# A hybrid encoder layer: the mixers' pieces put into the stream of dense products in twos, or alone after a time

## The chip, the cores and the metric

The kernel runs on one NeuronCore of a Trainium2 chip. The metric is the device time of one execution in microseconds (us). The core has TensorE (PE: matrix products; PEld is its weight load), VectorE (DVE), ScalarE (ACT), GpSimd (POOL) and SyncE (SP, which here issues most of the DMAs). They run their own queues of instructions and wait for each other by semaphores.

## What is computed

One layer of a streaming encoder, for a prompt of 1024 tokens and 8 samples of 16 tokens, 1152 columns in all, at a model width of 1024:

```python
def trunk_layer(x, mem_k, mem_v, ...):
    y, ... = hybrid_mixer(rms_norm(x, norm_mix_w), ...)     # x @ W_in -> 4 mLSTM + 4 gated-DeltaNet heads -> @ W_out
    x = x + y
    x = x + memory_cross_attention(rms_norm(x, norm_x_w), mem_k, mem_v, wq_x, wo_x)
    x = x + squared_relu_mlp(rms_norm(x, norm_ffn_w), w_ff1, w_ff2)

def hybrid_mixer(xn, ...):
    proj = xn @ w_in
    ...
    (C1, n1, m1), h = lax.scan(mlstm_chunk_step, carry0, ...)
    ...
    S1, o = lax.scan(gdn_chunk_step, S0, ...)               # delta rule: a triangular solve in each chunk
    ...
    y = jnp.concatenate([h_a, h_b], axis=-1) @ w_out
```

All is float32. The big ("dense") products are made of fp32r products of a high and a low part of each operand, three of them for one product; the mixers' own small products are plain fp32.

## The kernel before

The activations lie with features on partitions and the 1152 columns in three blocks of 384. A dense product of one chunk of 128 output features is `project` (line 377): for each block, `dense` (line 235) makes eight steps of three matmuls of 128x128 by 128x384 into one PSUM bank. A chunk thus has 24 dense steps, and its weights are loaded and split one chunk ahead (`chunks`, line 1902).

The order of the work is written out by a planner. `Driver` (line 72) holds a clock `t` and a list of tasks; a task is a Python generator that emits instructions and yields `(pe, delay)`: the time on TensorE that it has just emitted, and how long its next step should stay away until its inputs are there. `stream` (line 103) takes the dense steps one by one; each yields `3 * n / 2360.0` (line 257), which moves `t` on, and then `run_ready` (line 83) runs every task that is due. Such a step of a task is called a piece here. Where the dense stream itself can't go on, it yields WAIT, and `skip` (line 96) moves `t` to the next task that is due. Two things make it wait: a flag (`wait`, line 218) and slots. All long-lived tiles are slots of one pool of 34; `room_s` (line 149) holds a chunk until enough are free, with a reserve for heads that have started, and tasks poll in `room` (line 144) and `until` (line 223).

The building framework then orders the instructions of each engine itself, by priority (which is the order of emission, with `hp()` ahead) and by when it thinks an instruction's inputs are ready.

The stream of the stage that the change touches is one call (line 1994). In it come, after an opening of three chunks: for each head the projections of a delta-rule ("gdn") head, three chunks with a short convolution, and of an mLSTM head, three chunks, with the two heads' gate chunks some chunks later; then the memory keys (`mem_k`, line 1094, which waits for the flag `rm`) and values; then the first seven of eight chunks of W_out for block 0. As tasks run:
- `gates` (line 460): the gates' cumulative sums for all heads;
- `gdn` (line 681), one head after the other: 6 transposes (delay 0.5), a pause of 2.0, 9 score steps (0.4), pauses of 0.8 and 0.2, 3 transposes (0.4), a pause of 4.5, 15 steps of a substitution on DVE alone (`yield 0.0, 0.6`), pauses of 5.0 and 0.8, 6 steps of a block inverse (1.0 to 1.2), 6 steps of products with it (0.2 and 0.4), and the state pass over 9 tiles (steps of 0.8 and 0.4 in turn);
- `mlstm` (line 964), one head after the other, from when its three chunks are projected: 16 steps of transposes and scores (0.4 and 0.5), 13 of a state pass (0.2 to 0.6);
- `head_out` (line 937): the head's normalisation, three output transposes, once the gate chunk is there;
- `conv_act` (line 619): three steps after each convolution chunk;
- `mem_in` (line 1068), spawned two chunks ahead of `mem_k`: once nine slots are free, it loads the memory tokens (line 1077), splits and squares them in eight steps of delay 0.8 (lines 1083 to 1087), and sums and spreads the row factor; then it sets `rm`.

The last gate chunk frees 17 slots (line 665). PSUM has three banks for the dense products and five for the pieces (`psd`, `psm`).

Of the kernel before, what the change touches and what calls it, by code (L numbers as in the profile page):

```python
# [64 lines left out]
A_Q, A_S, A_P, A_T, A_X = 2.5, 0.5, 3.0, 1.5, 3.5  # L65
X_DELAY = (0.0, 9.5, 18.0)
WAIT, BREAK = -1.0, -2.0
MIX_ORDER = (4, 0, 5, 1, 6, 2, 7, 3)
ORDER = [("g", 0), ("m", 0), ("g", 1), ("m", 1), ("g", 2), ("m", 2), ("g", 3), ("m", 3)]


class Driver:
# [2 lines left out]

    def __init__(self):
        self.t, self.tasks, self.n, self.idle = 0.0, [], 0, 0

    def spawn(self, gen, delay=0.0):
        self.n += 1  # L80
        self.tasks.append([self.t + delay, self.n, gen])

    def run_ready(self):
        while True:
            ready = [k for k in self.tasks if k[0] <= self.t]
            if not ready:
                return
            k = min(ready, key=lambda k: k[1])
            try:
                pe, delay = next(k[2])  # L90
                self.t += pe
                k[0] = self.t + delay
            except StopIteration:
                self.tasks.remove(k)

    def skip(self):
        assert self.tasks, "nothing can run"
        self.idle += 1
        assert self.idle < 20000, [k[2].__qualname__ for k in self.tasks]
        self.t = max(self.t, min(k[0] for k in self.tasks))  # L100
        self.run_ready()

    def stream(self, steps):
        for x in steps:
# [7 lines left out]
class Kern:  # L112
# [31 lines left out]
    def room(self, n):  # L144

        while NSLOT - self.live < n:
            yield 0.0, 0.4

    def room_s(self, n):

# [72 lines left out]
    def until(self, *flags):  # L223

        while not all(f in self.done for f in flags):
            yield 0.0, 0.5

    def mm3(self, ps, lh, ll, rh, rl, start, stop, more=False):

# [707 lines left out]
    def head_out(self, ov, sc, r, hd):  # L937
# [7 lines left out]
        for g in range(3):  # L945
# [7 lines left out]
            nc.sync.dma_start(self.mixD[:, hd, s], gate[:, s])  # L953
            if hd == MIX_ORDER[-1] and g == 0:
                while 0 not in self.mix:
# [194 lines left out]
    def mix_in(self, b):  # L1150
# [13 lines left out]
        self.x1[b] = lambda k: x1t[k // 3][:, k % 3]  # L1164
        left = [k for k in MIX_ORDER if b or k != MIX_ORDER[-1]]
        for k in left:
# [16 lines left out]
    def wout(self, b, f):  # L1183
        w = yield
        if f == 0:
            yield from self.wait(f"mixin{b}{MIX_ORDER[0]}")
        x1 = self.x1[b]
        yield from self.dense(
            w, self.mix[b], lambda ps: self.nc.vector.tensor_tensor(x1(f), ps[:, :BW], x1(f), ALU.add),
            order=MIX_ORDER, need=(lambda k: f"mixin{b}{k}"))  # L1190
        if f == KT - 1:
            self.F(6)
            self.dr.spawn(self.norm_x(b))
# [218 lines left out]
    def wo(self, b, f):  # L1412
        w = yield
        yield from self.wait(f"oin{b}0")
        x1 = self.x1[b]
        yield from self.dense(
            w, self.o[b], lambda ps: self.nc.vector.tensor_tensor(x1(f), ps[:, :BW], x1(f), ALU.add),
            need=lambda k: f"oin{b}{k}")
        self.done.add(f"wo{b}{f}")
        if f == KT - 1:  # L1420
            self.F(6)
# [545 lines left out]
    def build(self):  # L1967
        tc, nc, A, dr = self.tc, self.nc, self.A, self.dr
        self.x1g, self.x1, self.x1t, self.xn2, self.q, self.o, self.rs16, self.mix = {}, {}, {}, {}, {}, {}, {}, {}
        self.xq, self.xo, self.hid, self.E, self.fs, self.keep = {}, ({}, {}), {}, {}, {}, 4  # L1970
        wout = lambda b: [(A["wout"][f], self.wout(b, f)) for f in range(KT)]
        PS = bass.MemoryType.PSUM
        with ExitStack() as ps:
            dense = ps.enter_context(ExitStack())
            self.pd = dense.enter_context(tc.tile_pool(name="psd", bufs=3, space=PS))
            self.pm = dense.enter_context(tc.tile_pool(name="psm", bufs=5, space=PS))
            with tc.tile_pool(name="m1", bufs=2) as m1:
                self.m1 = m1
                self.consts()
                self.xh = [self.S([P, T], F32R, "xh") for _ in range(KT)]  # L1980
                self.xl = [self.S([P, T], F32R, "xl") for _ in range(KT)]
                self.rB = self.S([P, T], F32, "rB")
                w0 = wout(0)
                seq = self.mixers()
                dr.stream(self.opening(seq[:3], seq[3][0]))
                nc.sync.dma_start(self.cst, A["cst"][:, C_NEGP:])
                zero = self.S([P, NT, 32], F32, "zero")
                nc.gpsimd.memset(zero, 0.0)
                nc.sync.dma_start(self.yD.rearrange("t s i -> s t i"), zero)
                self.F()  # L1990
                seq = seq[3:]
                seq[-4] = (seq[-4][0], self.also(seq[-4][1], [(self.mix_in(0), 0.0)]))
                w0[2] = (w0[2][0], self.also(w0[2][1], [(self.mix_in(1), 0.0)]))
                dr.stream(self.chunks(seq + w0[:7], w0[7][0]))
                self.finish(*(f"mix{k}" for k in range(8)))
                nc.sync.dma_start(A["pconv_o"], self.pconv)
                nc.sync.dma_start(A["sconv_o"], self.sconv)
            m4 = self.m4 = ps.enter_context(tc.tile_pool(name="m4", bufs=2))
            wq = lambda b: [(A["wq"][f], self.wq(b, f)) for f in range(KT)]
            wo = lambda b: [(A["wo"][f], self.wo(b, f)) for f in range(KT)]  # L2000

            def at(items, i, *tasks):
                items[i] = (items[i][0], self.also(items[i][1], [(t, 0.0) for t in tasks]))
                return items

            with tc.tile_pool(name="m2", bufs=2) as m2:
                self.m2 = m2
                self.reserve = 0
                seq = w0[7:] + wout(1) + at(wq(0), 0, self.mix_in(2), self.sample_loads())
                seq += wout(2) + wq(1) + at(wq(2), 0, self.o_in(0), self.o_in(1), self.o_in(2))  # L2010
                last = wo(2)
                seq += at(wo(0), 0, self.ff_in(0)) + at(wo(1), 0, self.ff_in(1), self.ff_split(0))
                dr.stream(self.chunks(seq, last[0][0]))
                self.finish(*(f"at{b}3" for b in range(NB)))
            m3 = self.m3 = ps.enter_context(tc.tile_pool(name="m3", bufs=2))
            full = [p for p in range(16) if p not in FIRST]
            units = [(p, (0,)) for p in FIRST] + [(p, (0, 1)) for p in full] + [(p, (1,)) for p in reversed(FIRST)]
            self.left = [sum(a in blocks for _, blocks in units) for a in range(2)]
            hid, ws = {}, []
            jobs = []  # L2020
            for i, (p, blocks) in enumerate(units):
                plain = i < len(FIRST)
                jobs.append(((A["wff1"][2 * p], A["wff1"][2 * p + 1]), 512, TWO if plain else UP,
                             self.up_plain(p, 0) if plain else self.up(p, blocks)))
            start = {len(jobs) - len(FIRST): [self.feed()]}
            for u, (d, idx) in enumerate(DOWN_UNITS):
                src = A[f"wd{u}"].rearrange("p q n -> p (q n)")
                n = len(idx) * P
                if u == len(DOWN_UNITS) - 4:
                    start[len(jobs)] = [self.plain_in(hid), self.plain_w(ws)]  # L2030
                jobs.append(((src[:, :2 * n], src[:, 2 * n:]), n, DOWN, self.down(u)))
            ff = self.seven(jobs, start)

            def warm():
                next(ff)
                yield 0.0, 0.0

            dr.stream(self.chunks(at(at(last, 0, self.ff_in(2), self.ff_split(1)), 6, warm())))
            dense.close()
            self.pf = ps.enter_context(tc.tile_pool(name="psf", bufs=4, space=PS))  # L2040
            dr.stream(ff)
            self.F(2)
            self.x1 = [lambda f, b=b: self.E[f].rearrange("p a n t -> p (a n t)")[:, b * BW:(b + 1) * BW]
                       for b in range(NB)]
            dr.stream(self.ff2_last(ws, hid))
            while dr.tasks:
                dr.skip()
# [121 lines left out]
```

## Time and profile before

| | us |
|---|---|
| median of three runs | 1833.7 (1833.43 to 1834.89) |
| the profiled execution | 1834.41 |
| its span, first to last instruction | 1832.6 |
| TensorE busy in the span | 1773.2 |
| DVE busy | 1236.7 |
| ScalarE busy | 788.5 |
| POOL busy | 444.2 |

In a timeline a row is a run of instructions of one kind on one engine: its start, its length, the engine, the line of the kernel, the operation, the tile written and those read, the shape, how many there are, and in brackets the idle time of the engine before it and what ended it. Matmuls are pipelined, so a matmul's length overlaps the next one's; the beat is read from the starts. A plain fp32 product of 128 columns shows as two instructions (two passes).

### The profile page before, as it was taken

The numbers are of one execution on the slowest core, as the hardware profiler recorded it, in microseconds if no ns is written. First come the engines' busy times: TensorE is split into PE (matmuls) and PEld (weight loads), VectorE is DVE, ScalarE is ACT, GpSimd is POOL, SyncE is SP. The second block draws the span as 40 slices with busy tenths as digits, with TensorE's granted clock in tenths as the row PEclk, the third lists the DMA queues.
The fourth block names the chain that finished last, engine by engine and source line by source line (L and its number), as shares of the span: only waits on it lengthen the run. The fifth ranks groups of instructions, "written<-read, shape, count | busy, mean of one in ns | idle before, by whom it ended". The sixth has DMA issues, their size and how long they took to land. (4 is left out here: it accounts for less than half of the span.)

```text
span 1832.6 us, 32932 instructions
## 1 busy us (share of the span) xinstructions
PE 1773.2 (97%) x12938; PEld 1718.5 (94%) x12938; DVE 1236.7 (67%) x2243; ACT 788.5 (43%) x1690; POOL 444.2 (24%) x415
## 2 busy tenths in 40 slices
PE   7999899999999999999999989999999899999997
PEld 6998899998999999988999989999999799999996
DVE  7877656765675667544676687555556777867886
ACT  6334324315225465445665444444445633433433
POOL 3023213122112202020002454222223332222213
PEclk9999999999999999999999999999999899999999
DMA  4111221121112476796144533433335834533512
GB/s 174 55 56 44 73 77 54 52 76 62 65 53 90 152 264 218 247 323 233 59 162 148 187 110 106 146 142 138 143 142 177 287 119 142 169 121 121 168 42 104
DMA packets 100706, 242.91 MB, mean 133 GB/s; under 512 B 24736, under 2 KB 48192, under 8 KB 100552
## 3 DMA queue, kind: packets, MB, share of 16 engines
q1 hardware_dynamic: 100256, 240.62, 38.7%
q8 instruction: 102, 1.67, 0.4%
q14 instruction: 52, 0.43, 0.1%
q10 hardware_dynamic: 296, 0.19, 0.0%
HBM read 182.87 MB, written 57.91 MB: 131 GB/s over the span
## 5 line engine op out<-in xcount | busy, mean ns | idle before, releaser
L231 PE MATMUL d<-xh,wh 128*128 128x384 f32 x944 | 342.1, 362 | 1.1 <-DVE k L458 0.6
L233 PE MATMUL d<-xh,wl 128*128 128x384 f32 x944 | 320.6, 340 | 0.3 <-DVE wl L212 0.3
L232 PE MATMUL d<-xl,wh 128*128 128x384 f32 x944 | 317.9, 337 | 0.0
L211 ACT CAST wh<-wr 128x1024 fp32r<-128x1024 f32 x120 | 126.0, 1050 | 244.5 <-PE d L232 190.8
L212 DVE TENSOR_TENSOR wl<-wr,wh 128x1024 fp32r<-128x1024 f32 x119 | 150.4, 1264 | 74.0 <-ACT wh L211 73.5
L231 PEld LDWEIGHTS d<-xh,wh 128*128 128x128 f32 x944 | 178.9, 190 | 7.3 <-issue 5.3
L232 PEld LDWEIGHTS d<-xl,wh 128*128 128x128 f32 x944 | 179.3, 190 | 1.6 <-issue 1.4
L233 PEld LDWEIGHTS d<-xh,wl 128*128 128x128 f32 x944 | 178.1, 189 | 0.8 <-DVE wl L212 0.6
L188 ACT CAST wh<-ws 128x512 fp32r<-128x512 f32 (+3 forms) x148 | 76.1, 537 | 132.1 <-issue 52.2
L188 ACT CAST wh<-wr 128x512 fp32r<-128x512 f32 (+4 forms) x121 | 68.9, 578 | 108.9 <-PE Z L232 38.1
L189 DVE TENSOR_TENSOR wl<-ws,wh 128x512 fp32r<-128x512 f32 (+3 forms) x148 | 95.3, 657 | 16.7 <-ACT wh L188 16.3
L231 PE MATMUL Y<-xqh,wh 128*128 128x288 f32 x348 | 104.2, 299 | 2.0 <-ACT wh L188 1.4
L233 PE MATMUL Y<-xqh,wl 128*128 128x288 f32 x348 | 104.1, 299 | 0.9 <-DVE wl L189 0.9
L232 PE MATMUL Y<-xql,wh 128*128 128x288 f32 x348 | 103.9, 299 | 0.0
L189 DVE TENSOR_TENSOR wl<-wr,wh 128x512 fp32r<-128x512 f32 (+4 forms) x121 | 87.9, 732 | 23.7 <-ACT wh L188 23.3
L231 PE MATMUL Y<-hh,wh 128*128 128x288 f32 x336 | 99.5, 296 | 0.4 <-DVE E L1789 0.3
L232 PE MATMUL Y<-hl,wh 128*128 128x288 f32 x336 | 99.0, 295 | 0.0
L233 PE MATMUL Y<-hh,wl 128*128 128x288 f32 x336 | 98.8, 294 | 0.0
L188 ACT CAST hh<-ht 128x1152 fp32r<-128x1152 f32 x53 | 61.1, 1157 | 80.8 <-DMA ht<-hD 32.9
L1512 POOL TENSOR_TENSOR ws<-wr 128x512 f32<-128x512 f32 (+3 forms) x37 | 43.1, 1164 | 189.9 <-DMA wr<-wd 109.5
L189 DVE TENSOR_TENSOR hl<-ht,hh 128x1152 fp32r<-128x1152 f32 x53 | 79.8, 1510 | 11.4 <-ACT hh L188 11.4
L231 PE MATMUL X<-xqh,wh 128*128 128x288 f32 x232 | 68.7, 296 | 7.9 <-ACT h L1652 7.9
(495 smaller groups left out, 5345.6 us busy)
## 6 DMA issues: line engine op xcount, KB each, us to landing
ht<-hD SPq DMA_DIRECT2D x42, 576.0 KB
hD<-h SPq DMA_DIRECT2D x39, 576.0 KB
wr<-wff SPq DMA_DIRECT2D x38, 512.0 KB
wr<-win SPq DMA_DIRECT2D x32, 512.0 KB
wr<-wout SPq DMA_DIRECT2D x24, 512.0 KB
wr<-wq SPq DMA_DIRECT2D x24, 512.0 KB
wr<-wo SPq DMA_DIRECT2D x24, 512.0 KB
wr<-wd SPq DMA_DIRECT2D x32, 384.0 KB
```

The costliest lines, as they stand in the source:

```text
L188: self.nc.scalar.copy(h, x)
L189: self.nc.vector.tensor_tensor(l, x, h, ALU.subtract)
L211: nc.scalar.copy(wh, raw)
L212: (nc.gpsimd if pool else nc.vector).tensor_tensor(wl, raw, wh, ALU.subtract)
L231: mm(ps, lhsT=lh, rhs=rh, start=start, stop=False, skip_group_check=more)
L232: mm(ps, lhsT=lh, rhs=rl, start=False, stop=False, skip_group_check=more)
L233: mm(ps, lhsT=ll, rhs=rh, start=False, stop=stop, skip_group_check=more)
L1512: self.nc.gpsimd.tensor_tensor(q[o], q[a], q[b], op)
```

## The change

`Driver` gets two numbers, `together` and `late`. `run_ready` now runs nothing until at least `together` tasks have a step of work that is due, or until one such step has been due for `late` units; then it runs all that is due, as before. A step that only polls (for slots or for flags, now marked by the common tuple `POLL`) runs at any time and does not count. `skip` runs all that is due, whatever the numbers. `together` is 2 and `late` 1.2 during the one stream of the mixers' stage, and 1 and 0.0 elsewhere, which is the rule of before. Polls for slots have a delay of 0.5 instead of 0.4.

```diff
--- before.py
+++ after.py
@@ -65,6 +65,7 @@
 A_Q, A_S, A_P, A_T, A_X = 2.5, 0.5, 3.0, 1.5, 3.5
 X_DELAY = (0.0, 9.5, 18.0)
 WAIT, BREAK = -1.0, -2.0
+POLL = (0.0, 0.5)
 MIX_ORDER = (4, 0, 5, 1, 6, 2, 7, 3)
 ORDER = [("g", 0), ("m", 0), ("g", 1), ("m", 1), ("g", 2), ("m", 2), ("g", 3), ("m", 3)]
 
@@ -75,21 +76,28 @@
 
     def __init__(self):
         self.t, self.tasks, self.n, self.idle = 0.0, [], 0, 0
+        self.together, self.late = 1, 0.0
 
     def spawn(self, gen, delay=0.0):
         self.n += 1
-        self.tasks.append([self.t + delay, self.n, gen])
-
-    def run_ready(self):
+        self.tasks.append([self.t + delay, self.n, gen, False])
+
+    def run_ready(self, go=False):
+
         while True:
             ready = [k for k in self.tasks if k[0] <= self.t]
+            work = [k for k in ready if not k[3]]
+            go = go or len(work) >= self.together or any(self.t - k[0] >= self.late for k in work)
+            if not go:
+                ready = [k for k in ready if k[3]]
             if not ready:
                 return
             k = min(ready, key=lambda k: k[1])
             try:
-                pe, delay = next(k[2])
+                step = next(k[2])
+                pe, delay = step
                 self.t += pe
-                k[0] = self.t + delay
+                k[0], k[3] = self.t + delay, step is POLL
             except StopIteration:
                 self.tasks.remove(k)
 
@@ -98,7 +106,7 @@
         self.idle += 1
         assert self.idle < 20000, [k[2].__qualname__ for k in self.tasks]
         self.t = max(self.t, min(k[0] for k in self.tasks))
-        self.run_ready()
+        self.run_ready(True)
 
     def stream(self, steps):
         for x in steps:
@@ -144,7 +152,7 @@
     def room(self, n):
 
         while NSLOT - self.live < n:
-            yield 0.0, 0.4
+            yield POLL
 
     def room_s(self, n):
 
@@ -223,7 +231,7 @@
     def until(self, *flags):
 
         while not all(f in self.done for f in flags):
-            yield 0.0, 0.5
+            yield POLL
 
     def mm3(self, ps, lh, ll, rh, rl, start, stop, more=False):
 
@@ -1988,10 +1996,12 @@
                 nc.gpsimd.memset(zero, 0.0)
                 nc.sync.dma_start(self.yD.rearrange("t s i -> s t i"), zero)
                 self.F()
+                dr.together, dr.late = 2, 1.2
                 seq = seq[3:]
                 seq[-4] = (seq[-4][0], self.also(seq[-4][1], [(self.mix_in(0), 0.0)]))
                 w0[2] = (w0[2][0], self.also(w0[2][1], [(self.mix_in(1), 0.0)]))
                 dr.stream(self.chunks(seq + w0[:7], w0[7][0]))
+                dr.together, dr.late = 1, 0.0
                 self.finish(*(f"mix{k}" for k in range(8)))
                 nc.sync.dma_start(A["pconv_o"], self.pconv)
                 nc.sync.dma_start(A["sconv_o"], self.sconv)
```

## Rows read from the trace of the kernel before

**Rows 1.** The page, part 1: busy time, share of the span, instructions.

```profile
PE 1773.2 (97%) x12938; PEld 1718.5 (94%) x12938; DVE 1236.7 (67%) x2243; ACT 788.5 (43%) x1690; POOL 444.2 (24%) x415
```

**Rows 2.** Windows: stretch, busy us and instructions by engine, granted clock, DMA share, GB/s.

```profile
60.00:240.00 180.00, 171.00 (x1287) 161.38 (x1286) 136.14 (x309) 65.29 (x211) 44.54 (x47) 0.97 0.17 52
219.00:227.00 8.00, 6.87 (x26) 6.54 (x27) 4.87 (x11) 3.57 (x26) 1.81 (x1) 0.57 0.41 140
```

**Rows 3.** Waits of TensorE, 52 to 700 us: us in total, times, longest.

```profile
PE ot L261 <- ACT junk L702: 4.7, 3, 2.7
PE p L1017 <- DVE k L995: 1.5, 2, 1.0
PE xb L794 <- ACT QT L789: 1.3, 2, 0.8
PE kt L261 <- ACT junk L702: 1.0, 2, 0.5
PE p L883 <- DVE W L880: 0.8, 1, 0.8
PE p L878 <- DVE Sg L888: 0.7, 1, 0.7
PE p L1017 <- DVE R L992: 0.7, 1, 0.7
...
PE cl L261 <- DVE cb L517: 0.6, 1, 0.6
```

**Rows 4.** Timeline of TensorE, 516 to 521 us: start, us, engine, line.

```profile
516.42 0.34 PE L231 MATMUL d<-xh,wh 128*128 128x384 f32 x1
...
516.95 0.38 PE L729 MATMUL kq<-up 128*128 128x128 f32 x2
517.17 0.39 PE L730 MATMUL kq<-up,up 128*128 128x128 f32 x2
...
520.83 0.38 PE L729 MATMUL kq<-up 128*128 128x128 f32 x2
```

**Rows 5.** Timelines of POOL, ScalarE and TensorE, 210 to 218 us.

```profile
210.43 0.81 POOL L677 TENSOR_TENSOR D<-D,cst 128x128 f32<-128x128 f32 x1 [6.75 <-DMA D<-rowD]
211.20 2.39 POOL L678 TENSOR_TENSOR D<-D,cst 128x1024 f32<-128x1024 f32 x1
...
213.62 0.69 ACT L723 ACTIVATE D<-D,cols 128x128 f32<-128x128 f32 x2 [1.95 <-POOL D L678]
...
215.51 0.25 ACT L702 ACTIVATE junk<-kt 128x128 f32<-128x128 f32 x1
...
217.56 0.52 PE L261 MATMUL ot<-cst,up 128*128 128x128 f32 x3 [2.69 <-ACT junk L702]
```

**Rows 6.** Timeline of TensorE, 146 to 150 us.

```profile
146.79 0.38 PE L1024 MATMUL p<-v,R 128*128 128x129 f32 x2
...
149.96 0.49 PE L1017 MATMUL p<-v,k 128*128 128x129 f32 x2 [1.03 <-DVE k L995]
```

**Rows 7.** Timeline of TensorE: first pieces of heads 0, 1 and 3, last of head 3.

```profile
101.23 0.50 PE L261 MATMUL kt<-cst,up 128*128 128x128 f32 x3
...
210.43 0.38 PE L261 MATMUL kt<-cst,up 128*128 128x128 f32 x2
...
504.67 0.38 PE L261 MATMUL kt<-cst,up 128*128 128x128 f32 x2
...
604.77 0.39 PE L892 MATMUL p<-Sg,up 128*128 128x128 f32 x2
```

**Rows 8.** Queue SP at 604 us; instructions by line on tiles mh and mf.

```profile
604.07 0.59 SPq L1077 DMA_DIRECT2D mf<-memT  x1
...
L231 PE MATMUL d<-mh,wh x64: 274/282/362, 627.7 to 650.1; 128*128 128x256 f32 x64
...
L1083 ACT ACTIVATE mh<-mf,prm x8: 493/495/509, 609.2 to 617.4; 128x256 fp32r<-128x256 f32 x8
...
L1085 ACT ACTIVATE mf<-mf x8: 399/418/419, 611.7 to 620.7; 128x256 f32<-128x256 f32 x8
```

## Prediction

> **What bounds the kernel now.** I read the page first: TensorE is busy for 97% of the span [rows 1], so this is a TensorE kernel and a change is worth what it does to TensorE's own time. The change acts between the opening and the end of the mixers, some 60 to 640 us, so I read that stretch with the windows view: TensorE stands still for 9.0 us of the 180 before 240 us [rows 2]. The waits view of TensorE alone says for what, in the whole stretch: the eight rows kept hold 11.3 us, and five more, none over 0.6, make it 13.4 [rows 3]. Beside them the clock is granted at 0.57 on average in 219 to 227 us, so for a part of it at the lower of its two levels; that costs 8.0 x 0.43 = 3.4 us [rows 2], just behind a wait of 2.69 us [rows 5]. So what any better placing of the pieces can win is about 13.4 + 3.4 = 17 us, 0.9%. All else in the stretch is matmuls that stay as they are.
>
> **What alternation itself costs.** The first guess would be that TensorE pays for each switch between the dense products (fp32r) and a piece (fp32), and that half as many switches save half of that. The row to ask is a stretch where it switches at a steady beat: the nine score steps of a delta-rule head, one dense step between each two [rows 4]. From 516.95 to 520.83 four beats take 0.970 us each. A dense step by itself is 0.53 (516.42 to 516.95), two passes of the fp32 product 0.22 (516.95 to 517.17), four of them 0.44: 0.97. The switch costs nothing that the row can show (below 0.01 us; even 300 of them would make 3 us, of which half could be saved). I take 0, bounds 0 and -1.5.
>
> **What the change does to a piece.** A step that waits alone now goes 1.2 planner units after it is due, and is run at the next dense step; a dense step counts 3 x 384 / 2360 = 0.488 units (line 257) and takes 0.53 us [rows 4]. A step with delay 0.4, which followed after one dense step, now follows after four (1.6 / 0.488, rounded up); with 0.5 four instead of two, with 0.6 four instead of two. Steps of nothing but DVE work (0.0, 0.6) count as pieces too, only POLL does not. So how often a step finds a partner decides. In a delta-rule head the first 22 steps (six transposes, nine scores, three transposes and four pauses) come while the mLSTM of the same head has not begun; they are alone. Counted out, they move by 6x2 + 2 + 9x3 + 3+2 + 3x3 + 2 = 57 dense steps, 30 us. Then the 29 steps of the mLSTM serve as partners, mostly for the substitution. They are spent when the state pass comes: some 22 steps, 2 or 3 dense steps later each, about 29 us, less what the nine steps of three convolutions lend. I count 45 to 50 us more for a head.
>
> **Where that room is.** The last head takes 504.67 to 604.77, 100 us; heads 1 and 3 start at 210.43 and 504.67, so a head has 147 us on average [rows 7]. 100 + 45 to 50 fits in, just, for heads 1 and 2: they are paced by the dense chunks of their own projections and a later end hides behind dense work. It does not fit for head 0 (101.23 to the start of head 1: 109 us) nor for head 3 (504.67 to the first product of mem_k at 627.7: 123 us) [rows 7, 8].
>
> **What is won.** Each wait below is a piece put before its input was there, and a later place removes it up to the shift.
> - Transposes waiting for a PSUM buffer that ScalarE has not yet read: 4.7 + 1.0 = 5.7 us [rows 3]. ScalarE stands at the exponentials of D, whose mask POOL ends at 213.59, and only then, at 215.51, reads the first transpose [rows 5]. The mask waited 6.75 us for a DMA, not for TensorE, so it does not move, while the transposes follow each other four dense steps apart instead of two: three, not six, are out by then, and five buffers do. Bounds 0 and -5.7; I take -5.7, since the shift of 2 x 0.53 per piece, over six pieces, exceeds the longest wait, 2.7.
> - The clock behind them: 3.4. Bounds 0 and -3.4, I take -3.4, since the fall comes straight behind the longest of these waits.
> - State pass, 0.8 + 0.7, and gates, 0.6: alone, so moved by 1.2: -2.1. The inverse's second product, 1.3, has a partner in half of the heads: -0.7.
>
> Sum -11.9, bounds 0 and -17.
>
> [...]
>
> **What is lost in head 0.** Where the mixers are late, slots are not freed, the next chunk stands at room_s, and skip runs everything due, without pairs, as before. The kernel before has one such place: 141 to 152 us. TensorE does not stop there, since the building framework moves dense matmuls of later steps between the pieces (of the 3.2 us from the piece at 146.79 to that at 149.96 it is idle for 1.03; most of the rest are dense matmuls), but pieces put this tightly wait: 1.5 + 0.7 for such products in all [rows 3, 6]. Head 0 gets a second stretch of the kind, heads 1 and 2 a short one at their end: 2.2 + 0.8 = +3. Bounds 0 and +10 (four long stretches). With a piece its DMAs move too (rows, inverse, states, all on SP); behind them on SP stand weight loads, issued a chunk of 12 us ahead of their use, which covers a shift of 1 to 2 us.
>
> **What is lost at the end.** mem_in needs nine slots. Before, head 3 frees them at its end: its DMA is issued at 604.07, ScalarE starts at 609.2, and mem_k starts at 627.7, straight behind the last piece of mem_in; there is no slack [rows 8]. With head 3 some 25 us late the slots come only with F(17), at the end of the last projection chunk. Then mem_in's chain lies bare: 5.1 us of DMA and eight steps of 0.50 + 0.42 on ScalarE, 12.5 us, until mem_k's first chunk can end [rows 8]. TensorE has in it what is left of head 3 (a round of the state pass is eight passes of 0.11, 0.9 us, in 2.1 by its delays: 5 to 6 us of the 12.5) and that chunk (eight of them take 627.7 to 650.1, 2.8 each): 12.5 - 5.5 - 2.8 = +4. Bounds 0 and, with mem_in's whole 23.6 us and the same cover, 23.6 - 8.3 = +15.
>
> **The sum.** -11.9 + 3 + 4 = -4.9 us against the profiled execution, 1834.4 (its span of 1832.6 and 1.8 around it), which lies 0.7 above the median of the three: 1834.4 - 4.9 - 0.7 = 1829 us, -0.26%. A measurement here can tell about 0.2%, 3.7 us.
>
> **The rivals.**
> - *The mixers fall behind (slower).* One mechanism: nearly every step is alone, the 1.2 adds up in a serial chain, and at the end mem_in and the rest of head 3 lie bare. Price: +14 there, +6 in head 0 and its like, -11.9 + 2 won: +10, 1844. It decides where head 3 grows from 100 us to more than 123; by my count it does, so only the cover is in doubt. For it: mem_k starts without slack. Against it: the dense matmuls that stand between the pieces at 146.79 and 149.96.
> - *The transposes wait all the same (slower).* The exponentials stand ahead of the squares in any order, and the pairs put a head's transposes and the last head's output transposes together, which fills the buffers again: the 9.1 stay, -4.9 + 9.1 = +4.2, 1838. Against it: half the pace of transposes.
> - *It does not do what it says (same).* Most steps go alone, and the framework that orders the instructions puts DVE steps and matmuls where it finds them ready, as it did at 146.79; what remains of gain and loss cancels: 1834, within 0.2%.
>
> **Chances.** Forecast 0.43 (its own range 1822 to 1831), mixers behind 0.21, transposes still waiting 0.10, no effect 0.26. Faster by over 0.2% 0.42, within 0.2% 0.27, slower 0.31. The range reaches down to the full -11.9 with little lost (1821) and up past the first rival (1846).
>
> **What would show it.** Right: the waits on L702 gone, the clock whole at 219 to 227 us, score steps four dense steps apart, the last state product of head 3 past 627 us, mem_in's DMA less than 20 us ahead of mem_k, TensorE idle around mem_k by 4 us. Wrong: the score steps keep their beat of 0.97 (no effect); the L702 waits stay; an idle of over 10 us ahead of mem_k; long waits of TensorE for state products.

## The result, and the profile after

The changed kernel takes 1854.1 us (median of 4 runs, 1853.6 to 1854.2), the kernel before 1834.1: a ratio of 1.0109, 95% interval 1.0096 to 1.0122. It is slower by 20 us where 1829 was forecast, and outside the range. The profiled execution took 1854.1 us with a span of 1852.1, so 19.5 more than the span before.

The page of the changed kernel, part 1 (busy time of each engine), to be held against [rows 1]:

```profile
PE 1779.7 (96%) x12938; PEld 1720.7 (93%) x12938; DVE 1238.3 (67%) x2243; ACT 792.7 (43%) x1690; POOL 451.0 (24%) x415
```

TensorE runs the same 12938 matmuls, is busy for 6.5 us more and stands still for 13.0 us more. The windows view says where. Its columns are the stretch, its length, the busy time of TensorE, of its weight load, of DVE, ACT and POOL, the granted clock, the share of the DMA engines and GB/s. First the kernel before, in four stretches (behind the opening, behind head 0, the middle, the end of the mixers):

```profile
52.00:172.00 120.00, 115.36 (x931) 108.59 (x929) 94.33 (x222) 43.92 (x129) 26.16 (x35) 0.99 0.18 54
172.00:240.00 68.00, 62.95 (x402) 59.57 (x402) 45.34 (x98) 23.71 (x84) 20.19 (x17) 0.95 0.16 51
240.00:600.00 360.00, 355.99 (x2983) 341.22 (x2982) 228.11 (x538) 124.22 (x374) 74.43 (x86) 1.00 0.22 70
600.00:670.00 70.00, 70.00 (x522) 68.79 (x521) 47.36 (x87) 38.34 (x72) 10.75 (x21) 1.00 0.53 180
```

The same stretches of the changed kernel, and three short ones in it:

```profile
52.00:172.00 120.00, 117.11 (x727) 113.21 (x726) 88.76 (x210) 41.91 (x119) 29.81 (x36) 0.99 0.17 52
172.00:240.00 68.00, 59.95 (x589) 54.70 (x588) 41.61 (x93) 27.23 (x94) 16.73 (x11) 0.92 0.18 55
240.00:600.00 360.00, 352.77 (x2898) 335.99 (x2897) 226.41 (x519) 120.63 (x346) 74.03 (x86) 1.00 0.21 67
600.00:670.00 70.00, 61.20 (x453) 56.92 (x452) 43.70 (x102) 30.88 (x75) 15.27 (x23) 0.95 0.42 145
...
184.00:191.00 7.00, 5.44 (x138) 4.87 (x139) 4.71 (x8) 3.32 (x7) 0.15 (x1) 0.51 0.29 82
...
228.50:232.00 3.50, 3.08 (x14) 3.08 (x15) 2.14 (x4) 1.04 (x7) 0.37 (x1) 0.51 0.16 56
...
648.40:655.20 6.80, 5.50 (x26) 5.50 (x27) 2.62 (x6) 0.78 (x3) 1.65 (x13) 0.50 0.44 113
```

At 600 to 670 us, where TensorE never stood still before, it is idle for 8.8 us, and for 6.8 us the granted clock is 0.50 instead of 1.00, which costs 3.4: 12.2 together, the larger part of the loss. Behind head 0 the idle time goes from 5.05 to 8.05 us. The one fall of the clock of before (3.4 us [rows 2]) is gone there, and two others have come, 3.4 us at 184 to 191 and 1.7 at 228.5 to 232, so 1.7 more: 4.7. In the other two stretches 8.6 us of idle become 10.1: 1.5 more. Together 18.4 of 19.5.

The 11.9 us that were to be won do not all lie in those two stretches. The waits on L702 of the kernel before, in the stretch behind head 0 (172 to 240 us) alone:

```profile
PE ot L261 <- ACT junk L702: 3.7, 2, 2.7
...
PE kt L261 <- ACT junk L702: 0.5, 1, 0.5
```

With the 0.7 of the state pass, which also lies there, and the clock's 3.4, that stretch held 8.3 of the 11.9, and the other two 3.6.

The waits of TensorE in the changed kernel, 52 to 720 us (in total, times, longest), which answer to [rows 3]:

```profile
PE ot L269 <- POOL up L949: 4.9, 3, 3.1
PE p L891 <- DVE W L888: 4.2, 5, 1.3
PE xa L795 <- DVE Y0T L790: 3.6, 1, 3.6
PE ot L269 <- POOL wr L146: 3.6, 1, 3.6
PE st L998 <- DVE R L1000: 2.8, 3, 1.0
PE d L241 <- DVE wl L220: 1.7, 1, 1.7
PE p L886 <- DVE Sg L896: 1.3, 2, 0.9
PE d L240 <- DVE ml L1092: 1.1, 1, 1.1
```

The waits on ScalarE's squares (L702 before, L710 now) are gone, as forecast, but not for the reason given. ScalarE's last exponentials of head 1 and its first square in the changed kernel:

```profile
219.00 0.68 ACT L731 ACTIVATE D<-D,cols 128x128 f32<-128x128 f32 x2
...
223.83 0.26 ACT L710 ACTIVATE junk<-kt 128x128 f32<-128x128 f32 x1
```

The exponentials are done at 219.7 us, before the head's first transpose (222.53); in heads 2 and 3 they are done 6 us before it. POOL's mask has hardly moved (213.86, 353.73 and 500.14 us, before 210.43, 356.33 and 501.02), but the whole head comes 7 to 12 us later, past its exponentials. So the fewer buffers of transposes "out by then" were not put to the test here. In place of these waits stand waits on POOL's scaling of a head's outputs, on the state pass's W and on one inverse.

How far the heads move is read from TensorE's timeline (start, length, line): first, from the kernel before, the last state product of head 1; then, from the changed kernel, the first transposes of heads 1, 2 and 3, the last state products of heads 1 and 3, and two of the score steps.

```profile
316.17 0.39 PE L892 MATMUL p<-Sg,up 128*128 128x128 f32 x2
...
222.53 0.38 PE L269 MATMUL kt<-cst,up 128*128 128x128 f32 x2
...
366.15 0.39 PE L900 MATMUL p<-Sg,up 128*128 128x128 f32 x2
...
366.90 0.49 PE L269 MATMUL kt<-cst,up 128*128 128x128 f32 x3
...
513.66 0.38 PE L269 MATMUL kt<-cst,up 128*128 128x128 f32 x2
...
528.77 0.38 PE L737 MATMUL kq<-up 128*128 128x128 f32 x2
...
531.31 0.38 PE L737 MATMUL kq<-up 128*128 128x128 f32 x2
...
641.17 0.39 PE L900 MATMUL p<-Sg,up 128*128 128x128 f32 x2
```

Head 1 takes 144 us (222.53 to 366.15) instead of 106 (210.43 [rows 7] to 316.17), head 2 takes 146 instead of 101, and head 3 takes 127.5 instead of 100 and ends at 641 instead of 605. Each head now starts less than 1 us after the last state product of the head before (222.31, 366.15, 512.90); before there were 14 to 44 us between them. So heads 1 and 2 have used up their room as well, and 9 of the 36 us by which head 3 ends late are its later start.

What that does at the end is in the timelines of POOL and TensorE there (in brackets the idle time just before and what ended it):

```profile
646.66 2.99 POOL L949 TENSOR_TENSOR up<-up,soy 128x1152 f32<-128x1152 f32 x1 [0.76 <-DVE soy L192]
...
649.70 2.18 PE L269 MATMUL ot<-cst,up 128*128 128x128 f32 x9 [3.55 <-POOL wr L146]
...
660.02 0.39 PE L241 MATMUL d<-mh,wl 128*128 128x256 f32 x1 [1.69 <-DVE wl L220]
```

The last head's outputs must be scaled on POOL before TensorE can transpose them. Before, that lay under the last projection products, the transposes (613.96) following the last state product by 9 us [rows 7]. Now TensorE has only mem_k's short products (256 columns) left and stands at the transposes for 3.55 us (the view names POOL's next instruction, a small memset; the scaling itself ends at 649.65, 0.05 before the transposes start). The clock falls at 648.4, and the next weights' split on DVE is late by 1.69 us.

### The profile page after: what moved, and what is told of

Its sections match the earlier page's. It is cut to its first block, busy times and chain, and to the rows that moved or that the text cites. A ratio compares the mean times of both kernels' runs of the same rounds, so it can differ in the third digit from the quotient of the medians.

```text
span 1852.1 us, 32916 instructions
## 1 busy us (share of the span) xinstructions
PE 1779.7 (96%) x12938; PEld 1720.7 (93%) x12938; DVE 1238.3 (67%) x2243; ACT 792.7 (43%) x1690; POOL 451.0 (24%) x415
## 5 line engine op out<-in xcount | busy, mean ns | idle before, releaser
L1520 POOL TENSOR_TENSOR ws<-wr,wr 128x512 f32<-128x512 f32 (+3 forms) x37 | 57.2, 1546 | 82.6 <-DVE wl L197 82.6
```

The lines of the kernel that those rows point to most:

```text
L1520: self.nc.gpsimd.tensor_tensor(q[o], q[a], q[b], op)
```

## The experiments

Two theories at first. Theory A: what costs is the lateness, because it adds up along a head, and only where the head then has no room: behind head 0 and at the end. Theory B: the pairs cost by themselves, wherever they stand. Each kernel was timed beside the kernel before, whose median lay at 1833.6 to 1834.7 us; a ratio is to that.

**Pieces one at a time from head 3 on** (in `gdn`, once the head before has ended):

```diff
             yield from self.until(f"gdn{h - 1}")
+        if h == 3:
+            self.dr.together, self.dr.late = 1, 0.0
```

> The changed kernel with one edit: from the start of head 3's delta rule on, pieces go one at a time again. Theory A (two places): the change lengthens every head by some 45 us, and it costs where a head then has no room: at the end (600 to 670 us: 8.8 us more of idle TensorE and 3.4 us of lower clock, 12.2 together) and behind head 0 (172 to 240 us: 3.0 idle and 1.7 of clock, 4.7). By A this kernel gives back about 10 of 19.5 us: 1844, with under 3 us of idle in 600 to 670. Theory B (the pairs): two pieces back to back wait for each other wherever they stand, so each of the four heads costs 5: 1849.

Measured: 1844.4 us, 1.0058 (1.0046 to 1.0071). The end alone gives back 9.8 us. The windows view of this kernel there:

```profile
600.00:670.00 70.00, 67.58 (x496) 64.98 (x495) 45.93 (x95) 33.55 (x72) 13.31 (x23) 1.00 0.48 169
```

2.4 us of idle instead of 8.8, and the clock whole (1.00). As A said.

**One at a time until head 1** (the line in `build` that sets 2 and 1.2 is moved to the start of head 1):

```diff
-                dr.together, dr.late = 2, 1.2
...
+        if h == 1:
+            self.dr.together, self.dr.late = 2, 1.2
```

> The changed kernel with pieces one at a time until head 1's delta rule starts, in pairs from there to the end. Theory A: 4.7 us of the 19.5 go, those behind head 0: 1849, with the clock fall at 184 us gone and the end as bad as before. Theory B: a quarter of 19.5: 1849 too, but with the end's idle of 8.8 us smaller only by its share.

Measured: 1851.4 us, 1.0092 (1.0079 to 1.0106): 2.7 us back, where both theories said 5, the clock whole (1.00) from 172 to 240 us, and the end as bad as in the changed kernel:

```profile
600.00:670.00 70.00, 61.34 (x446) 58.02 (x445) 44.44 (x101) 30.73 (x73) 15.37 (x23) 0.93 0.43 147
```

The stretch behind head 0 itself gives back more than the time shows: it is idle for 3.3 us instead of 8.05 and loses nothing to the clock instead of 5.1. Against that the profiled execution loses 1.7 us more at 52 to 172 us, 1.7 more of clock at the end (0.93 instead of 0.95), and 3.4 more of clock in the opening (0.90 instead of 0.97 over the first 52 us), which the edit does not touch. So 2.7 is a low price for head 0.

**Pairs in heads 1 and 2 alone** (both edits):

> Both edits: pairs for heads 1 and 2 alone, the two heads that have room. Theory A: of the 19.5 us some 15 go: 1838 to 1840, the rest being the 3 us of idle between 240 and 600. My first reckoning (these heads win the waits on the transposes and lose nothing) gives 1828 to 1832. Theory B: two heads of four, 1844.

Measured: 1841.8 us, 1.0048 (1.0036 to 1.0061). 12.3 us are back, nearly what the two edits gave singly (9.8 + 2.7): two separate places. But 8 us remain, where theory A had 4 to 6 and my first reckoning wanted a gain. Heads 1 and 2 turn out to have no room either: in this kernel they run from 209.82 to 361.93 and from 362.68 to 508.53, each head again less than 1 us behind the one before, and head 3 ends at 613.8 instead of 604.8. Of the loss 2.5 us of idle at 600 to 670 and 1.0 at 670 to 720 stand behind that late end, where TensorE was never idle before.

**The polling alone** (0 units of allowed lateness, so nothing waits for a partner; what is left is 0.5 for 0.4 in `room`):

```diff
-                dr.together, dr.late = 2, 1.2
+                dr.together, dr.late = 2, 0.0
```

> The changed kernel with the allowed lateness at 0, so that no piece waits for a partner; what is left of the change is that a task that looks for slots asks every 0.5 planner units instead of 0.4. Both theories: 1834, no difference from the kernel before (within 2 us). If it is slower, part of the loss is the asking and not the waiting.

Measured: 1835.2 us, 1.0008 (0.9999 to 1.0017). No difference that can be told.

**mem_in late, and nothing else** (in the kernel before):

```diff
     def mem_in(self):
+        yield from self.until("gate3")
         yield from self.room(7 + MR)
```

> The kernel before with one edit: mem_in waits for the flag of the last projection chunk, as the changed kernel makes it wait in effect; no pairs, no later pieces, head 3 ends as before at 605 us. It prices the bare chain of mem_in alone. Theory A (two places): of the 12.2 us that the changed kernel loses at 600 to 670, most are this chain: 8 to 12 us, 1842 to 1846, with the clock falling once near 650. My first reckoning put the term at 4: 1838. If it is within 2 us of before, the loss at the end belongs to head 3's own pieces.

Measured: 1842.2 us, 1.0041 (1.0027 to 1.0055), 8 us slower with every head on time. What TensorE waited for at 600 to 720 us (the kernel before has no wait there):

```profile
PE d L231 <- ACT wh L211: 2.0, 2, 1.6
PE d L233 <- DVE wl L212: 2.0, 3, 0.8
```

Hardly for mem_in's own output, then, but 4.0 us for mem_k's weights: their splits run on ScalarE and DVE, where mem_in's steps now stand among them (1.7 us of the waits, to 636 us; the other 2.3 come at 645 us, when mem_in's steps are over). The clock falls at 646 to 652 us, 1.7 us (0.98 on average at 600 to 670 us), and mem_k takes 32.4 us (626.7 to 659.1) instead of 22.4 [rows 8]. These waits do not make up the 8 us: 4.5 us of it are longer busy time of TensorE, which no view here explains.

**Only the transposes later** (in the kernel before):

```diff
+        gap = (0.5, 1.7, 1.7, 1.0)[h]
...
-            yield 0.33, 0.5
+            yield 0.33, gap
```

(twice, for k and q.)

> The kernel before with one edit: the six transposes of k and q of a head follow each other after 1.7 planner units instead of 0.5 in heads 1 and 2 and after 1.0 in head 3; nothing else is later. It prices what I booked as won: 5.7 us of waits on L702 and 3.4 of clock. My reckoning: 1834 - 5.7 - 3.4 = 1825, at the least the 3.7 us that head 1's place holds (2.7 of wait, part of the clock). The rival, that the squares behind the exponentials decide and not the pace: 1834 and the waits on L702 still there.

Measured: 1831.3 us, 0.9984 (0.9975 to 0.9993): 2.9 us faster, a third of what I had booked. The waits on L702 are all gone and the clock is whole (1.00) at 172 to 240 us. But other waits have grown; the longest of this kernel:

```profile
PE p L884 <- DVE W L881: 2.2, 3, 1.0
PE kt L261 <- DVE kd L709: 1.7, 1, 1.7
PE p L879 <- DVE Sg L889: 1.5, 2, 0.8
```

One new wait of 1.7 for a transpose's buffer, now behind a DVE step, and the state pass from 0.8 and 0.7 [rows 3] to 2.2 and 1.5.

**Every step late by itself, no pairs** (0.6 units for each step, and `together` at 1):

```diff
-            go = go or len(work) >= self.together or any(self.t - k[0] >= self.late for k in work)
+            go = go or len(work) >= self.together
...
-                k[0], k[3] = self.t + delay, step is POLL
+                k[0], k[3] = self.t + delay + (0.0 if step is POLL else self.late), step is POLL
...
-                dr.together, dr.late = 2, 1.2
+                dr.together, dr.late = 1, 0.6
```

> The changed kernel with the rule taken apart: every step is due 0.6 planner units later than it asks, half of the 1.2, and none waits for a partner. Theory A (lateness is what costs, through heads that outlast their room): heads 1 and 2 take some 150 us, head 3 is later still, 1850 to 1862. Theory B (the pairs cost, lateness by itself hides behind dense work): 1834 to 1838.

Measured: 1853.4 us, 1.0101 (1.0085 to 1.0116). Lateness without a single forced pair loses as much as the change, as A said; B falls.

**Twice the lateness, and a quarter of it** (2.4 and 0.3 for 1.2):

> The changed kernel with 2.4 instead of 1.2 units of allowed lateness. Theory A: heads 1 and 2 have no room left either (147 us were filled to 144 already), so they too stand blocked at their ends, some 4 us each, and the end is later still: 1860 to 1866. Theory B: the number of pairs hardly changes, so 1852 to 1856.

Measured: 1860.3 us, 1.0139 (1.0122 to 1.0155), the lower edge of what A gave, and not what B did.

> The changed kernel with 0.3 instead of 1.2 units of allowed lateness. Theory A: each step is at most one dense step late, a head grows by some 10 us, head 3 still ends late for mem_in, about half of the loss at the end and behind head 0: 1842 to 1846. Theory B (pairs): few pairs are left, 1836 to 1838.

Measured: 1841.3 us, 1.0039 (1.0025 to 1.0053), just under the 1842 that A gave. So 0, 0.3, 1.2 and 2.4 units make 1835, 1841, 1854 and 1860: the first 0.3 costs 6 us already. That fits a chain, in which every step pays, and not the number of pairs. The end of the stage shows it:

```profile
600.00:670.00 70.00, 64.05 (x454) 61.24 (x454) 42.68 (x82) 32.41 (x66) 9.45 (x20) 0.98 0.50 176
```

Head 3 takes 113 us here instead of 100 and ends at 614.8, and 6.0 us of idle and 1.7 of clock stand at the end. At 172 to 240 us this kernel wins: 1.6 us of idle and the whole fall of 3.4. (The 6 is by the medians, of four runs here; the profiled one loses 3.4 us more than the kernel before to the clock in the opening, which the edit does not touch.)

**The state pass singly** (on top of the kernel with pairs in heads 1 and 2):

```diff
+        on = self.dr.together
+        self.dr.together, self.dr.late = 1, 0.0
         oS = U
...
         self.done.add(f"gdn{h}")
+        if on == 2:
+            self.dr.together, self.dr.late = 2, 1.2
```

> The kernel with pairs in heads 1 and 2 alone (it took 1841.8, 8 us more than before) with one more edit: in the state pass of these heads pieces go one at a time. Theory A, carried on: the rest of that loss sits in the state pass, which grew from 24.5 us to 42 a head, so that its products meet the 3.2 us DVE steps of the next head's convolutions (TensorE waits 4.5 us for W there) and its end stands blocked for slots. Then 1835 to 1837, with the wait for W at 1 to 2 us and no fall of the clock near 516. If the loss is spread over all pairs, 1840.

Measured: 1850.2 us, 1.0087 (1.0073 to 1.0100). Not 5 us less but 8 more: this part of the theory falls. The state pass is short again, so the head's outputs come at another time: the rule pairs them with the next head's transposes while ScalarE is still at that head's exponentials. (The changed kernel makes such pairs too, at 375 us, but its exponentials of that head are done by 361.) ScalarE, DVE and TensorE at the start of head 2 in this kernel:

```profile
364.62 1.85 ACT L733 ACTIVATE D<-D,cols 128x128 f32<-128x128 f32 x6
...
366.37 1.03 ACT L219 CAST wh<-wr 128x1024 fp32r<-128x1024 f32 x1
...
367.43 1.23 DVE L220 TENSOR_TENSOR wl<-wr,wh 128x1024 fp32r<-128x1024 f32 x1 [1.66 <-ACT wh L219]
...
369.04 0.61 DVE L964 SCALAR_TENSOR_TENSOR z<-ot,whalf,z 128x384 f32<-128x384 f32 x1
...
369.71 0.55 PE L269 MATMUL kt<-cst,up 128*128 128x128 f32 x3 [2.75 <-DVE z L964]
```

Read it upward: TensorE wants a buffer for the next transpose; it is freed by the DVE step on an output (369.04); that stands behind a weight split (367.43), which waits for ScalarE's cast (366.37), which stands behind six exponentials (364.62). Nothing in that chain reads what the exponentials write; the cast starts as the last of them ends (366.47); that it would have come earlier without them is argued, not shown. TensorE waits 2.75 us here and 2.81 once more at head 3, at 521.71 us. Theory C, then: pairs that match an output with a transpose fill the five PSUM buffers.

**The same, with outputs and transposes kept apart:**

```diff
+        if h > 1:
+            yield from self.until(f"mix{3 + h}")
         k2, q2, v2 = r[4 + h], r[h], r[8 + h]
```

> The last kernel (pairs in heads 1 and 2, their state passes singly, 1850.2) with one more edit: heads 2 and 3 start only after the previous head's three output transposes are out. In the last kernel the pairing rule put each output transpose together with a transpose of the next head, and TensorE waited 8.4 us there (5.6 for the DVE step that reads an output, 2.8 for ScalarE's squares). Theory C (the pairs fill the five PSUM buffers whose readers stand behind ScalarE's exponentials; my second rival): these 8.4 us go but for about 1, and a head 3 that starts 4 us later costs 2 to 3 at the end: 1843 to 1846. If the transposes are not the cause, the time stays at 1850 or rises with the later head: 1850 to 1854.

Measured: 1839.5 us, 1.0028 (1.0018 to 1.0038): 10.7 us back, more than the 8.4 of waits. Head 2 starts 6.3 us later than in the last kernel (369.65 instead of 363.37), but head 3 starts 2.5 us earlier (513.84 instead of 516.38), not later as the expectation had it. From 360 to 530 us, where the kernel without this edit waits for DVE's z (5.6) and ScalarE's squares, the only long wait left is

```profile
PE ot L269 <- POOL up L957: 2.1, 1, 2.1
```

So it was the outputs and the transposes together that cost that kernel these 10.7 us. The edit both parts them and starts head 2 later, so it does not tell whether the pair or its moment matters. In the changed kernel itself no such wait is among the rows.

**The transposes once more** (2.4, 1.2 and 0.7 for heads 1, 2 and 3, in the kernel before):

> The kernel before with the transposes of k and q spaced by 2.4 units in head 1, 1.2 in head 2 and 0.7 in head 3 (the spaced kernel had 1.7, 1.7 and 1.0 and took 1831.3). Head 1 holds the longest wait (2.7 us) and the fall of the clock at 219 us, and the spaced kernel left 1.66 us of wait there; head 3 has no room before mem_in, and 1.1 us of idle came back there. Theory A: 1829 to 1831, a little under the spaced kernel.

Measured: 1830.8 us, 0.9984 (0.9975 to 0.9992), 3.2 us faster than the kernel before and not to be told from the first spaced kernel. These two are the versions that beat both kernels, and they form no pairs.

## Why the prediction was wrong

Three steps of the sum failed. "What is won" counted a wait that is taken away as time that is won. "What is lost in head 0" had one more blocked stretch of the old kind, 2.2 us, where 13 us of new waits and clock came. And "what is lost at the end" left out the clock and the outputs of head 3: 12.2 instead of 4. By stretches, booked and measured (idle time and clock together):

| us | booked | measured |
|---|---|---|
| behind head 0, 172 to 240 | -8.3 + 2.2 | +4.7 |
| end, 600 to 670 | +4 | +12.2 |
| the other two stretches | -3.6 + 0.8 | +1.5 |

The measured ones make 1834.4 + 18.4 = 1853 against the 1854 of the profiled execution. By its own steps:

- **What alternation costs, nothing:** held. The score steps now follow each other after 2.54 us (528.77 to 531.31), which is their own 0.44 and four dense steps of 0.53. A pair costs TensorE what its pieces cost alone: one group of three transposes with two dense steps takes 1.39 us (366.90 to 368.29), a pair of groups with two dense steps 1.71 (374.92 to 376.63), 0.32 more, and a group by itself is 0.33:

```profile
374.92 0.49 PE L269 MATMUL ot<-cst,up 128*128 128x128 f32 x3
375.25 0.49 PE L269 MATMUL kt<-cst,up 128*128 128x128 f32 x3
...
376.63 0.49 PE L269 MATMUL ot<-cst,up 128*128 128x128 f32 x3
```

- **A head grows by 45 to 50 us:** right for head 2 (45), somewhat less for head 1 (38), and 27 for head 3.
- **Where the room is:** right for heads 0 and 3, and mem_in's DMA is issued 11 to 13 us ahead of mem_k (616.1 and 618.0; mem_k from 629.3), as the views of mf and mh show. Heads 1 and 2, though, did not fit "just": they fill what they have to the last microsecond, and head 3 inherits 9 us.

```profile
L1085 SPq DMA_DIRECT2D mf<-memT x2: 431/1128/1826, 616.1 to 618.0; - x2
...
L239 PE MATMUL d<-mh,wh x64: 274/282/415, 629.3 to 670.9; 128*128 128x256 f32 x64
```

- **What is won, -11.9:** this step failed. Most of the waits that I named did go (L702 from 5.7 to 0, xb from 1.3 to 0, the fall of the clock at 219 us), those on L702 with some luck, because the whole head came behind its exponentials. But I let a removed wait count as time won and never asked what comes next in that place. The state pass, of which I said -1.5, went from 1.5 to 5.5 (4.2 + 1.3). The spaced kernels price the largest term by itself: 9.1 booked (5.7 of waits and 3.4 of clock), about 3 real, though there all the waits on L702 are gone, or all but 1 us. In the first of them the buffers worked as I had it: the squares still stand behind the exponentials (in head 1 the first of them at 215.85 us, behind three exponentials from 214.97), and at the slower pace TensorE waits for none of them. The trace of before gave a warning: DVE is busy for 67% of the span [rows 1], so a piece that is moved off one peak can meet another.
- **Head 0, +3:** far too small. What was waited for at 172 to 240 us before is gone there, so all of the new 8.05 us of idle and 5.1 of clock, 13 us, are head 0's late end; only against the old waits is it 4.7. The mechanism named was a blocked chunk, in which pieces put tightly wait. The pieces do come tightly: head 0's state pass, from its first to its last product on Sg, takes 16 us (206.06 to 222.31), where it took 22 before (173.82 to 195.98) and takes 38 in head 1. That fits pieces which wait for no partner; that a chunk stood blocked is argued from it, no row shows it. And the waits are not of the kind of [rows 6]: one is for an inverse (3.6 us) that stands behind the convolution steps of the next head on DVE, one for the scaling of the outputs on POOL (3.1).
- **The end, +4:** the place and the lateness were right, the term was 12.2. I priced mem_in's chain against TensorE's cover and there it was nearly right: the one wait of the changed kernel for mem_in's output is 1.1 us, since head 3's pieces do cover. (With head 3 on time mem_in's lateness alone costs 8 us, 4.0 of it in waits for the weights' splits.) I left out what else becomes bare: the scaling and the transposes of head 3's outputs (3.55), the weight splits (1.69), and the clock, which fell to 0.50 in the wait of 3.55 us and cost 3.4. I had counted the clock among the gains and never among the losses.
- **The rival** "the mixers fall behind" had the sign and the mechanism, and said 1844. Its loss at the end, +14, came out at 12.2; its +6 "in head 0 and its like" was too small, and it booked -9.9 as won like the forecast. Its chance of 0.21 was too low for the same reason.
- **The second rival**, transposes paired with outputs, is not what slowed this kernel, but it is real: it appeared when the state pass was made short, and parting the two gave 10.7 us back.

What stays open: a part of the 8 us of the kernel with pairs in heads 1 and 2 alone. Its profile has 4.1 us more of idle TensorE (waits for W 4.5 us instead of 0.8, for POOL's scaling 2.8 instead of 0) and 4.0 more of busy time. Most of the idle part has its place (3.5 at 600 to 720, 3.0 at 240 to 600, against 1.9 less at 172 to 240); the busy part has none. The three largest groups of dense matmuls hold 345.2, 321.8 and 318.8 us in it and 342.1, 320.6 and 317.9 before, with the same counts and the same mean clock. In the trace a dense matmul's length overlaps the next one (0.34 us each, their starts 0.17 apart), so this may be waits too short to show as idle; that is argued, not shown. No single edit has undone it.

## What to carry to other kernels

Before delaying small work so that it packs better, count how far the delay adds up along the chain it belongs to, and look for the place where that chain has no slack; here 0.3 units a step, less than one dense step, cost 6 us. Look also at the heads that seem to have room: their lateness is handed on to the next one. A wait that is removed is won only if nothing else comes due at the new place: price it by moving that one piece alone. And give a long idle stretch of TensorE the price of the clock too: in the changed kernel each of the three waits of 3.1 to 3.6 us had a fall of the clock from 1.00 to 0.50 with it, 1.7 to 3.4 us (in the kernel with the state pass singly the dense matmuls behind the wait of 2.81 us, up to 525.84, take 0.34 us as they did ahead of it).

## What the runs showed of the hardware that was not expected

In these rows a long DVE step that starts beside a running POOL step takes up to 3.21 us instead of 1.23, and a short POOL step beside a long DVE step 1.33 instead of 0.46. In the kernel with pairs in heads 1 and 2, DVE's last step of a convolution, POOL's mask and TensorE's state product:

```profile
350.27 3.21 DVE L634 SCALAR_TENSOR_TENSOR up<-up,y 128x1024 f32<-128x1024 f32 x1
...
350.01 2.39 POOL L686 TENSOR_TENSOR D<-D,cst 128x1024 f32<-128x1024 f32 x1
...
354.08 0.46 PE L893 MATMUL p<-W,kd 128*128 128x128 f32 x2 [1.62 <-DVE W L890]
```

and the same DVE step with the short part of the mask, when DVE came first, in the kernel with the state pass singly:

```profile
359.67 1.23 DVE L634 SCALAR_TENSOR_TENSOR up<-up,y 128x1024 f32<-128x1024 f32 x1 [0.66 <-ACT up L631]
...
359.88 1.33 POOL L685 TENSOR_TENSOR D<-D,cst 128x128 f32<-128x128 f32 x1 [6.22 <-DMA D<-rowD]
```

1.23 us becomes 3.21 when POOL was first, and TensorE waits 1.62 us for W behind it; where DVE was first, POOL's small step takes 1.33 us instead of 0.46 (the same step at 349.59 us in the first of the two kernels, with no long DVE step beside it) and ends 0.3 us after the DVE step. The kernel before and the changed one show the same: of the 24 DVE steps of this line and shape in the two, 17 take 1.19 to 1.23 us, and the seven that start while a POOL step over 1024 or 1152 columns runs take 2.17 to 2.98 and end 1.08 to 1.09 us after it (in the changed kernel 355.02 + 2.66 = 357.68, POOL's mask 354.15 + 2.44 = 356.59). So in these rows most of the DVE step comes after the POOL step's end; why, no row shows.
